# A hybrid mLSTM and retention block on one core: first norm in two parts, scan pieces issued by an account of VectorE and ScalarE

## The chip, the cores and the metric

The kernel runs on one core of one Trainium2 chip. The metric is the device time of one execution in microseconds (us). The median of three runs of the kernel before is 1547.75 us (1546.34 to 1549.2). The engines are named as in the profile: PE is TensorE, DVE is VectorE, ACT is ScalarE, POOL is GpSimd and SP is SyncE, whose queue issues most of the loads and stores.

## What is computed

One layer over a stream of 16 learned meta tokens and 1024 frames of width 1024, in float32. The input is normalised, projected, run through four mLSTM heads (0 to 3) and four retention heads (4 to 7), and projected back; a gated feed-forward part with causal convolutions follows. Cut to what matters:

```python
def token_mixer(u, ...):                       # u: normalised stream
    proj = up @ w_in                           # q, k, v, gate o, input and forget gates
    qk = silu(causal_dwconv(concat(ml_q, ml_k), ml_conv_w))
    h_ml = mlstm_chunkwise(q, k, v, li, lf)    # heads 0-3: decay tables from the gates
    h_ml = sigmoid(ml_o) * head_norm(h_ml)
    h_rt = retention_chunkwise(rotary(rt_q), rotary(rt_k), rt_v, log_gamma)   # heads 4-7
    h_rt = silu(rt_g) * head_norm(h_rt)
    return concat(h_ml, h_rt) @ w_out

h = concat(meta, x)
h = h + token_mixer(rmsnorm(h, norm_mix_g), ...)
u = rmsnorm(h, norm_ffn_g)
h = h + (silu(causal_dwconv(u @ w_up)) * (u @ w_gate)) @ w_down
return rmsnorm(h, norm_final_g)[:, N_META:]
```

## The kernel before

**Dense products.** Each float32 operand of the large products is split into a rounded high part and a low remainder, and a product is three matmuls: high by high (L729), low by high (L730), high by low (L731). `parts` makes the split of a weight: a cast on ACT (L334), a subtraction on DVE (L339). The projections use a seven-product scheme on halves of both operands; the halves of the stream and their sums (S1 to S4, made by `usum` and split by `usplit`, L1551) are its left sides, sums of weight halves its right sides. PSUM banks of a finished product are added into their targets by `evac` (L793): ACT copies or DVE adds (L795, L797, L799). The pairs of letters in the names are the kind of projection: pq for queries and keys, pv for values of a pair of heads, po for the output gate (its target is sig), x and y for the two output halves.

**The stages.** The stream's first norm and head 4's own q, k and v come first (`first_norm`, `v4_group`, `q4_group`), in column ranges of 144, 128, 256, 272 and 256 (r = 0 to 4). Then the order of heads is 4, 0, 1, 2, 3, 5, 6, 7; the dense steps of one head run beside the scan of the head before it. Then follow w_out (about 720 us on), the up and gate products (about 880 on) and the down product.

**The scan.** Each head has nine chunks (16 columns, then eight of 128). `scan_a` makes the scores s of a chunk and from them kw (ACT) and the masked scores pt (DVE); `scan_b` makes the state update u and the output n, and with DVE the next state C. After a third of the chunks, `post_steps` takes the statistics for the head norm (bn, mv, z), scales the values (ACT, into v4lo and v4hi for head 4), and transposes them (tr); DVE multiplies by the gate (mx) and SP stores the result. For heads 0 to 3 the decay tables A1 and A2 are loaded from a scratch array by `tables_load` (L908), and `tables_tasks` (L924) adds the mask on DVE (L931, L932) and takes the exponential on ACT. `qk_tasks` makes convolution, silu or rotary of the next head's q and k.

**What sets the order.** The program deals these pieces out between the dense steps. `watch` keeps an account of each engine's time, `load`, from the sizes of the instructions issued. `slot` issues one dense step of 12 matmuls, first letting the waiting generators (`front`, `pend`) go on by a step, then taking pieces from the list `side`. A piece that uses TensorE has a condition, and is taken when the instructions that it rests on have been issued: their names are in the set `done`. Pieces that are left at the end of a stage are issued by `drain` without dense steps between them. Tile's scheduler makes the final order of each engine from this. Raw weights are loaded on SP's queue by jobs into four slots; `w_unit` (L474) makes sums of two row blocks of w_out and stores them for later.

**The first norm.** `rms` (L665) multiplies the squared stream by a column of ones to get sums per column (pca), takes the root on ACT and the reciprocal on DVE (rcola), and spreads the result over the partitions by a product with the identity (pra). `first_norm` (L692) squares and adds, calls `rms`, scales the stream by it and splits it into u11h, u11l and so on.

## Time and profile before

| | |
|---|---|
| median of three runs | 1547.75 us |
| the profiled execution | 1548.18 us, span 1546.4 us |
| PE busy | 1497.8 us (97%), 9917 matmuls |
| DVE busy | 1080.8 us (70%) |
| ACT busy | 766.1 us (50%) |
| POOL busy | 74.3 us (5%) |
| HBM | 178.05 MB read, 67.15 MB written |

The rows shown further down are of the profiled execution. A row of the view of waits reads: engine, what waited, what it waited for, microseconds in total, times, longest. A row of the timeline has start, duration, engine, line, operation, output and inputs, shape, count, and in brackets the idle time ahead of it with what ended it. Tile numbers are left out of names there: tr, n, u, s, C, A are those of whichever head is at work. Busy time of PE is modelled, since matmuls are pipelined.

### The profile page before, as it was taken

Reading aid. Unit: us, or ns where it says so; the run is one execution under the profiler, and the core shown is the slowest. Engines: PE = TensorE matmul, PEld = TensorE weight load, DVE = VectorE, ACT = ScalarE, POOL = GpSimd, SP = SyncE. Lnnn points to the kernel's source line nnn. Section 1 sums busy time; section 2 is a strip of 40 time slices with the busy share of each in tenths; the row PEclk is TensorE's granted clock in tenths of the full one; section 3 lists DMA queues with packets and bytes.
Section 4 is the critical chain, followed back from the end, with each engine's and each line's share of the span. In section 5 each row is a group of like instructions: output and inputs, shape, how many; then the busy total and the mean of one; then the engine's idle time right before and its main releaser. Section 6 shows DMA issues by size and latency. Waiting matters only on the chain.

```text
span 1546.4 us, 25487 instructions
## 1 busy us (share of the span) xinstructions
PE 1497.8 (97%) x9917; PEld 1353.0 (87%) x9917; DVE 1080.8 (70%) x2112; ACT 766.1 (50%) x1464; POOL 74.3 (5%) x133
## 2 busy tenths in 40 slices
PE   6999799999999999999999999999999999999997
PEld 5999689999889999997888988999999999888887
DVE  7885667667667567755768778666666666778657
ACT  5564565565555446543445455444444444434443
POOL 1000000000000000000000001222220000000000
PEclk9999899999999999999999999999999999999999
DMA  6132146223533354589333228887773223933313
GB/s 243 42 110 71 41 112 216 78 87 116 186 112 101 103 186 166 196 309 337 103 109 132 87 78 241 206 210 199 190 185 89 82 82 128 381 110 112 98 43 110
DMA packets 104585, 223.79 MB, mean 145 GB/s; under 512 B 10520, under 2 KB 33760, under 8 KB 104288
## 3 DMA queue, kind: packets, MB, share of 16 engines
q1 hardware_dynamic: 95872, 199.02, 38.7%
q0 software_dynamic: 8448, 23.07, 7.5%
q8 instruction: 77, 1.26, 0.3%
q14 instruction: 44, 0.36, 0.1%
q10 hardware_dynamic: 144, 0.07, 0.0%
HBM read 178.05 MB, written 67.15 MB: 159 GB/s over the span
## 4 chain that ended last, share of the span: by engine, by line
PE 80%; DVE 4%; DMA 4%; ACT 3%; issue 1%; SPq 0%; DVEq 0%; ACTq 0%
PE pdx L731 3%; PE pdx L730 3%; PE pdx L729 3%; PE pup_x L730 2%; PE pup_x L731 2%; PE pga_x L729 2%; PE pup_x L729 2%; PE pga_x L730 2%; PE pga_x L731 2%; PE pdy L731 2%; PE pdy L730 2%; PE pdy L729 2%; PE pwx L731 2%; PE pwx L729 2%; PE pwx L730 2%; PE n L1366 2%
## 5 line engine op out<-in xcount | busy, mean ns | idle before, releaser
L628 ACT CAST hi_up<-raw_up 128x512 fp32r<-128x512 f32 (+1 forms) x52 | 36.4, 719 | 107.4 <-PE pga_z L730 61.1
L629 DVE TENSOR_TENSOR lo_ga<-fraw_ga,hi_ga 128x512 fp32r<-128x512 f32 (+1 forms) x52 | 41.8, 808 | 38.8 <-ACT hi_ga L628 38.6
L729 PE MATMUL pup_x<-uh_g,hi_up 128*128 128x256 f32 (+1 forms) x240 | 67.2, 283 | 1.2 <-ACT uh_g L1688 1.2
L730 PE MATMUL pup_x<-ul_g,hi_up 128*128 128x256 f32 (+1 forms) x240 | 67.4, 282 | 0.1
L629 DVE TENSOR_TENSOR lo_up<-raw_up,hi_up 128x512 fp32r<-128x512 f32 (+1 forms) x52 | 41.3, 809 | 37.4 <-ACT hi_up L628 36.6
L731 PE MATMUL pup_x<-uh_g,lo_up 128*128 128x256 f32 (+1 forms) x240 | 66.4, 282 | 0.0
L629 DVE TENSOR_TENSOR lo_d<-rd,hi_d 128x1024 fp32r<-128x1024 f32 (+1 forms) x34 | 37.7, 1112 | 32.8 <-ACT hi_d L628 32.7
L628 ACT CAST hi_ga<-fraw_ga 128x512 fp32r<-128x512 f32 (+1 forms) x52 | 36.4, 719 | 46.5 <-PE pup_z L730 22.7
L731 PE MATMUL pdx<-uh_d,lo_d 128*128 128x512 f32 (+1 forms) x156 | 57.9, 375 | 0.0
L730 PE MATMUL pdx<-ul_d,hi_d 128*128 128x512 f32 (+1 forms) x156 | 57.8, 374 | 0.0
L628 ACT CAST hi_d<-rd 128x1024 fp32r<-128x1024 f32 (+1 forms) x34 | 32.3, 959 | 49.3 <-PE pdy L730 32.5
L731 PE MATMUL pdy<-uh_d,lo_d 128*128 128x512 f32 x132 | 51.9, 393 | 0.0
L730 PE MATMUL pdy<-ul_d,hi_d 128*128 128x512 f32 x132 | 51.7, 392 | 0.0
L729 PE MATMUL pdx<-uh_d,hi_d 128*128 128x512 f32 (+1 forms) x156 | 48.5, 372 | 0.0
L729 PE MATMUL pdy<-uh_d,hi_d 128*128 128x512 f32 x132 | 47.9, 389 | 0.0
L729 PE MATMUL pga_x<-uh_g,hi_ga 128*128 128x512 f32 x120 | 47.5, 396 | 0.0
L730 PE MATMUL pga_x<-ul_g,hi_ga 128*128 128x512 f32 x120 | 47.5, 396 | 0.0
L729 PEld LDWEIGHTS pup_x<-uh_g,hi_up 128*128 128x128 f32 x240 | 45.3, 189 | 2.3 <-ACT uh_g L1688 1.4
L731 PE MATMUL pga_x<-uh_g,lo_ga 128*128 128x512 f32 x120 | 47.1, 393 | 0.0
L730 PEld LDWEIGHTS pup_x<-ul_g,hi_up 128*128 128x128 f32 x240 | 45.4, 189 | 1.0 <-DVE ul_g L1689 0.3
L731 PEld LDWEIGHTS pup_x<-uh_g,lo_up 128*128 128x128 f32 x240 | 44.7, 189 | 0.8
L509 POOL DMA_DIRECT2D wsd<-w_down_d x33 | 19.7, 733 | 471.6 <-DVE s2up L1916 471.2
(1688 smaller groups left out, 5779.7 us busy)
## 6 DMA issues: line engine op xcount, KB each, us to landing
raw_up<-w_up_d SPq DMA_DIRECT2D x22, 512.0 KB, 4.3
fraw_ga<-w_gate_d SPq DMA_DIRECT2D x22, 512.0 KB, 4.4
acts<-cv SPq DMA_DIRECT2D x44, 256.0 KB, 4.3
wsd<-w_down_d POOLq DMA_DIRECT2D x44, 256.0 KB, 6.8
rd<-wsd SPq DMA_DIRECT2D x22, 512.0 KB, 3.5
raw_w<-w_out_d SPq DMA_DIRECT2D x20, 512.0 KB, 5.6
wsw<-raw_w SPq DMA_DIRECT2D x32, 256.0 KB, 2.0
raw_m<-w_out_d SPq DMA_DIRECT2D x14, 512.0 KB, 4.5
```

What stands on the lines that cost most here:

```text
L509: dep(G.dma_start(x, y), last["pace"], True)
L628: AC.copy(hi[:, o:o + n], x)
L629: V.tensor_tensor(lo[:, o:o + n], x, hi[:, o:o + n].bitcast(F32), ALU.subtract)
L729: m.append(PE.matmul(pt, ah, xh_, start=first and k == 0, stop=False, skip_group_check=True))
L730: PE.matmul(pt, ah, xl_, start=False, stop=False, skip_group_check=True)
L731: m.append(PE.matmul(pt, al, xh_, start=False, stop=last and k == n - 1, skip_group_check=True))
L1366: PE.matmul(pn[:L, :nv], pt[:L, :L], v, start=True, stop=c == 0)
```

## The change

It has these parts.

1. **The first norm.** `first_norm` is cut in two: `norm_sums` (squares, column sums, root, reciprocal) and `norm_split` (spread, scale, split), and `rms` into `rms_sums` and `rms_rows`. The sums of a range are called one group of products ahead of its scaling. A range with a remainder takes one root and one reciprocal for all its columns instead of two; the second range gives its eight squares to TensorE unsummed.
2. **Head 4's values.** In `v4_group` the high part of the stream goes through both parts of the weights before its low part is used, and the second range's sums can be called between.
3. **Splits.** The subtractions of S3 and S4 in `usplit` run on GpSimd instead of DVE.
4. **The first `w_unit`** moves from ahead of head 4's gate to a place behind it.
5. **The issue rule.** `done` holds, with each name, the time on the account at which DVE and ACT are through with it; a piece is taken when PE's account has reached it. `tr` is such a name for the bank of the transposes. Waiting generators in `pend` pause while DVE or ACT is more than 3 us ahead of PE's account. A change of the activation table is charged 1.3 us to ACT. `tables_tasks` waits until PE's account is 9 us behind `tables_load`.

```diff
+    TABLES = ("Sqrt", "Sigmoid", "Silu", "Exp")
+    table = [None]
     def watch(ins):
...
+        if nm == "Activation":
+            f = ins.func.name if hasattr(ins, "func") else "Copy"
+            if f in TABLES and f != table[0]:
+                table[0] = f
+                load[nm] += 1.3
...
             for g in list(q):
+                if q is pend and not rush[0] and max(load["DVE"], load["Activation"]) - load["PE"] > 3:
+                    break
                 if next(g, pend) is pend:
...
-    done = set()
+    class Ready(dict):
+        def add(self, key):
+            self[key] = max(load["DVE"], load["Activation"]) + 0.3
+        def discard(self, key):
+            self.pop(key, None)
+        def can(self, *keys):
+            return all(k in self and (rush[0] or load["PE"] >= self[k]) for k in keys)
+    done = Ready()
...
+        done["tr"] = load["DVE"] + 0.9
...
-                while "meta" in done:
+                while "meta" in done or dealt[0] and not done.can("tr"):
                     yield
...
-        if k == 0:
-            ask(js)
...
-                if k:
-                    ask(js, True)
+                ask(js, True)
...
-    for f in w_units(1):
-        f()
-    u_fm("o", 4, *v_units(0, 0))
+    u_fm("o", 4, *v_units(0, 0), *w_units(1))
...
+    def norm_sums(r):
...
         if r < 2:
-            V.tensor_tensor(sq[1], xs[1], xs[1], ALU.mult)
+            m = V.tensor_tensor(sq[1], xs[1], xs[1], ALU.mult)
+            if r:
+                after(m, last["scale"])
...
+        if r == 1:
+            ss = [x[:, k] for x in sq for k in range(4)]
+        else:
+            V.tensor_tensor(sq[0], sq[0], sq[1], ALU.add)
+            V.tensor_tensor(sq[0][:, 0:2], sq[0][:, 0:2], sq[0][:, 2:4], ALU.add)
+            ss = [sq[0][:, k] for k in range(2)]
+        norms[r] = xs, rms_sums(ss[0], 0, n, f"a{r}", ..., "tr", ss[1:])
...
-        for i, j in ((0, 0), (1, 0), (0, 1)):
+        for i, j in ((0, 0), (0, 1), (1, 0)):
+            if i and between:
+                between()
...
+        tabs["at"] = load["PE"]
...
         def make():
+            while not rush[0] and load["PE"] < tabs["at"] + 9:
+                yield
...
+        done.add(("pre", h, c))
...
-            return lambda: {("qk", h, int(c > 4))} | ({("tab", h)} if h < H else set()) <= done and not (h == 7 and "meta" in done)
+            return lambda: done.can(("qk", h, int(c > 4)), *([("tab", h)] if h < H else [])) and not (h == 7 and "meta" in done)
...
-            return lambda: (h, c) in pre and (set(turn) <= done if c == 0 else ("n", h, c - 1) in done)
+            return lambda: (h, c) in pre and done.can(("pre", h, c), *(turn if c == 0 else [("n", h, c - 1)]))
...
-    first_norm(0)
+    norm_sums(0)
     v0_split()
+    norm_split(0)
+    v4_group(1, next(ring0), lambda: norm_sums(1))
     need(("q4", 0), 1)
-    v4_group(1, next(ring0))
+    norm_split(1)
     v4_group(0, next(ring0))
-    first_norm(1)
     v4_group(2, next(ring0))
-    first_norm(2)
+    norm_sums(2)
...
-            V.tensor_tensor(l_, part(x, i), h_.bitcast(F32), ALU.subtract)
+            (G if nm in ("S3", "S4") else V).tensor_tensor(l_, part(x, i), h_.bitcast(F32), ALU.subtract)
```

How the instructions move is shown at three places; a row has the line, the operation, output and inputs, shape and count, and lines are numbered by each kernel's own text. First TensorE at the end of head 4's scan, where pv0x1 and pv0y0 are dense products, u4, s4 and n4 the scan's, and tr4_1 the transposes of its second third. Before:

```order
L731 MATMUL pv0x1_1606<-hi_vp0_4_0_1823,uS3l_856 128x256
L1364 MATMUL u4_7_1593<-v4hi_207,kw4_7_1566 128x256
L1317 MATMUL s4_8_1589<-qT4_920,kT4_921 128x128
L1366 MATMUL n4_7_1595<-v4hi_207,pt4_7_1559 128x256
L1368 MATMUL n4_7_1595<-C4_6_1569,qT4_920 128x256
L1366 MATMUL n4_8_1621<-v4hi_207,pt4_8_1591 128x256
L1368 MATMUL n4_8_1621<-C4_7_1600,qT4_920 128x256
L1421 MATMUL tr4_1_0_1704<-cs_73,v4lo_206 128x128
L1421 MATMUL tr4_1_0_1704<-cs_73,v4hi_207 128x128 x2
L1421 MATMUL tr4_1_1_1708<-cs_73,v4lo_206 128x128
L1421 MATMUL tr4_1_1_1708<-cs_73,v4hi_207 128x128 x2
L729 MATMUL pv0y0_1653<-hi_vp0_5_0_1907,uS4h_883 128x256
```

and with the change, where the first rows are those around the first transposes and the dots stand for dense products alone:

```order
L1403 MATMUL n4_7_1556<-v4hi_207,pt4_7_1488 128x256
L1405 MATMUL n4_7_1556<-C4_6_1512,qT4_908 128x256
...
L761 MATMUL pv0x1_1620<-lo_vp0_2_0_1683,uS2h_611 128x256
L1458 MATMUL tr4_1_0_1638<-cs_73,v4lo_206 128x128
L762 MATMUL pv0x1_1620<-hi_vp0_2_0_1682,uS2l_612 128x256
L1458 MATMUL tr4_1_0_1638<-cs_73,v4hi_207 128x128
L760 MATMUL pv0x1_1620<-hi_vp0_2_0_1682,uS2h_611 128x256
...
L1403 MATMUL n4_8_1583<-v4hi_207,pt4_8_1536 128x256
L1405 MATMUL n4_8_1583<-C4_7_1562,qT4_908 128x256
...
L1458 MATMUL tr4_1_1_1667<-cs_73,v4lo_206 128x128
L1458 MATMUL tr4_1_1_1667<-cs_73,v4hi_207 128x128 x2
```

The run of scan products and transposes is broken up by 15 dense products behind n4_7, 16 more ahead of n4_8 and 18 more ahead of tr4_1_1.

Second DVE where head 1 gets its table A1_1, while head 0's gate product (po0, into sig) is emptied out of PSUM. Before:

```order
L931 TENSOR_TENSOR A1_1_2495<-A1_1_2495,mask_118 128x16
L339 TENSOR_TENSOR lo_q1_1_0_2448<-raw_q1a_2292,hi_q1_1_0_2447 128x512 x2
L416 TENSOR_TENSOR raw_q1a_2292<-raw_q1a_2292 128x512
L1383 BN_STATS bn0_7_2411<-v0_01_2138 128x6
L799 TENSOR_TENSOR sig_110<-sig_110,po0x0_2202 128x256
L932 TENSOR_TENSOR A1_1_2495<-A1_1_2495,mask_118 128x1024
L417 TENSOR_TENSOR raw_q1a_2292<-raw_q1a_2292,raw_q1b_2352 128x512
L799 TENSOR_TENSOR sig_110<-sig_110,po0x1_2236 128x256
L1384 BN_AGGR mv0_2_2396<-bn0_7_2411 128x2
L1355 MEMSET mv1_0_2973 128x2
L799 TENSOR_TENSOR sig_110<-sig_110,po0y0_2263 128x258
```

and with the change:

```order
L832 TENSOR_TENSOR sig_110<-sig_110,po0y1_2221 128x256
L1372 TENSOR_TENSOR pt0_8_2487<-s0_8_2485,A1_0_1642 128x128
...
L1437 SCALAR_TENSOR_TENSOR z0_1_2515<-z0_1_2515,mv0_1_2324 128x3
L1414 SCALAR_TENSOR_TENSOR C0_7_2520<-C0_6_2460,dec_115,u0_7_2510 128x257
L967 TENSOR_TENSOR A1_1_2616<-A1_1_2616,mask_118 128x16
L1420 BN_STATS bn0_7_2524<-v0_01_2088 128x6
L507 TENSOR_TENSOR raw_w9_2470<-raw_w9_2470,raw_w1_2468 128x512
L1443 RECIPROCAL z0_1_2515<-z0_1_2515 128x3
L968 TENSOR_TENSOR A1_1_2616<-A1_1_2616,mask_118 128x1024
L1421 BN_AGGR mv0_2_2509<-bn0_7_2524 128x2
L1444 SCALAR_TENSOR_TENSOR mv0_1_2324<-mv0_1_2324,z0_1_2515 128x3
L832 TENSOR_TENSOR rawq_102<-rawq_102,pq1y0_2602 128x264
```

The last evacuation of po0 now stands ahead of the mask's two additions, and the next evacuation behind them is one of pq1.

Third TensorE at the start, where pca is a column sum, pra the spread root, and pv4 head 4's values. Before:

```order
L673 MATMUL pca0_224<-cs_73,sqr0_132 16x1 x2
L673 MATMUL pca0_224<-cs_73,sqr0_132 128x1 x2
L685 MATMUL pra0_233<-cs_73,rcola0_223 128x16
L685 MATMUL pra0_233<-cs_73,rcola0_223 128x128
L767 MATMUL pv4_1_271<-w0hiq_106,u11h_124 128x264 x4
L767 MATMUL pv4_1_271<-w0hik_107,u12h_126 128x264 x4
L755 MATMUL pv4_0_298<-w0raw0_104,ug_117 32x264 x4
L767 MATMUL pv4_1_271<-w0hiq_106,u11l_125 128x264 x4
```

and with the change:

```order
L688 MATMUL pca0_220<-cs_73,sqr0_132 128x1 x4
L700 MATMUL pra0_231<-cs_73,rcola0_219 128x16
L700 MATMUL pra0_231<-cs_73,rcola0_219 128x128
L688 MATMUL pca1_268<-cs_73,sqr0_132 128x1 x4
L800 MATMUL pv4_1_248<-w0hiq_106,u11h_124 128x264 x4
L688 MATMUL pca1_268<-cs_73,sqr1_133 128x1 x4
L800 MATMUL pv4_1_248<-w0hik_107,u12h_126 128x264 x4
L800 MATMUL pv4_1_248<-w0lo0_108,u11h_124 128x264 x4
```

The second range's sums, now eight products instead of two, stand around the first group of values instead of behind it.

66 lines of the change are left out of this document (37 added, 29 removed).

## The prediction

> **What bounds the kernel now.** I read the head of the page first, then TensorE's busy time in stretches of the span, then what it waited for, then the clock in the stretches behind a wait. The profiled execution took 1548.18 us, 0.43 above the median of the three runs; its span is
>
> ```profile
> span 1546.4 us, 25487 instructions
> ```
>
> so 1.8 us lie outside it. By stretches (length, then busy time and instructions of PE, its weight loads, DVE, ACT, POOL; then PE's granted clock, DMA share and GB/s):
>
> ```profile
> core 0: us, PE busy (x) PEld busy (x) DVE busy (x) ACT busy (x) POOL busy (x), PEclk, DMA share, GB/s
> 0.00:20.00 20.00, 9.34 (x53) 6.91 (x54) 12.30 (x32) 11.70 (x19) 5.64 (x8) 1.00 0.96 326
> 20.00:40.00 20.00, 17.45 (x131) 16.80 (x131) 19.43 (x46) 9.85 (x18) 0.00 (x0) 0.91 0.40 152
> 40.00:80.00 40.00, 40.00 (x342) 39.09 (x341) 34.48 (x53) 22.05 (x36) 3.36 (x2) 1.00 0.13 37
> ...
> 150.00:180.00 30.00, 21.58 (x129) 18.62 (x127) 21.27 (x49) 19.22 (x36) 0.11 (x1) 0.83 0.14 45
> ...
> 222.00:235.00 13.00, 8.72 (x60) 7.93 (x59) 8.11 (x22) 10.68 (x22) 0.18 (x1) 0.93 0.44 161
> ...
> 300.00:320.00 20.00, 18.08 (x127) 17.22 (x126) 14.05 (x38) 15.22 (x30) 0.74 (x2) 0.91 0.18 54
> ...
> 395.00:410.00 15.00, 11.92 (x83) 11.35 (x82) 9.45 (x21) 11.20 (x21) 0.00 (x0) 0.89 0.53 166
> ...
> 720.00:740.00 20.00, 16.45 (x68) 12.51 (x67) 13.67 (x24) 4.81 (x7) 0.00 (x0) 0.91 0.64 219
> ...
> 960.00:1500.00 540.00, 540.00 (x3066) 473.07 (x3065) 365.71 (x552) 233.72 (x397) 50.81 (x72) 1.00 0.54 154
> ...
> sum 1546.40, PE 1497.84 PEld 1352.98 DVE 1080.78 ACT 766.11 POOL 74.33; mean PE 74.89 PEld 67.65 DVE 54.04 ACT 38.31 POOL 3.72
> ```
>
> TensorE sets the time: 1497.84 of 1546.4 us busy, and not idle at all from 960 to 1500. A change that leaves its products alone can win only the 48.6 us of idle and what is run at a low clock behind it. The change reorders two places: the first norm (10.66 + 2.55 us idle up to 40 us) and the scan of the heads, where 8.42, 4.28, 1.92 and 3.08 us are idle in four short stretches, 17.7 us together. The 3.55 at 720 to 740 stand in a part whose order on TensorE stays as it was. In those four stretches it waited for:
>
> ```profile
> PE tr L1421 <- ACT v4lo L1412: 3.8, 1, 3.8
> PE tr L1421 <- DVE mx L1429: 2.6, 1, 2.6
> PE n L1366 <- ACT v4hi L1379: 1.4, 1, 1.4
> ...
> PE pq1y L729 <- ACT sig L795: 2.0, 1, 2.0
> PE po0x L729 <- DVE sig L799: 1.6, 1, 1.6
> ...
> PE pq2x L729 <- DVE rawk L799: 1.9, 1, 1.9
> ...
> PE pq3y L729 <- ACT sig L795: 1.8, 1, 1.8
> PE pq3x L729 <- DVE sig L799: 1.3, 1, 1.3
> ```
>
> The first three are the end of head 4's scan: the last scan products and the transposes (tr) of its output follow one another with nothing dense between, so each waits out the chain of the other engines. The other five are dense products that wait for a PSUM bank which DVE or ACT has not emptied. What DVE did instead, at the second stretch, by its timeline and, for the other two, by its waits:
>
> ```profile
> 218.66 0.17 DVE L931 TENSOR_TENSOR A<-A,mask 128x16 f32<-128x16 f32 x1 [3.94 <-DMA A<-scr]
> ...
> 222.97 1.23 DVE L932 TENSOR_TENSOR A<-A,mask 128x1024 f32<-128x1024 f32 x1 [1.65 <-DMA A<-scr]
> ...
> 225.15 0.42 DVE L799 TENSOR_TENSOR sig<-sig,po0y 128x258 f32<-128x258 f32 x1
> ```
> ```profile
> DVE A L931 <- DMA A<-scr: 2.9, 1, 2.9
> ...
> DVE A L931 <- DMA A<-scr: 2.7, 1, 2.7
> ```
>
> DVE stood still for the decay table of the next head, with the evacuations of L799 queued behind it. And after each gap TensorE's clock was about half for a while:
>
> ```profile
> 174.35:178.57 4.22, 4.21 (x20) 4.22 (x21) 2.60 (x7) 3.87 (x6) 0.00 (x0) 0.51 0.13 47
> ...
> 233.16:236.40 3.24, 3.24 (x14) 3.24 (x15) 1.12 (x2) 2.86 (x6) 0.00 (x0) 0.50 0.76 229
> ...
> 315.26:318.80 3.54, 3.54 (x19) 3.28 (x19) 2.36 (x7) 3.54 (x12) 0.18 (x1) 0.55 0.00 0
> ...
> 403.90:406.50 2.60, 2.60 (x13) 2.60 (x13) 1.63 (x3) 1.27 (x3) 0.00 (x0) 0.50 0.56 180
> ```
>
> Length times (1 − clock) gives 2.07 + 1.62 + 1.59 + 1.30 = 6.6 us, which the busy share hides. The four places cost 17.7 + 6.6 = 24.3 us.
>
> **The scan's new issue rule.** A piece of the scan is now put out only when the account of DVE and ACT says that its inputs are done, and not by the fact that their instructions were issued. At the end of head 4 the new order has 15 dense products between its seventh n and the first transpose, 16 more before the last n and 18 more before the last transposes, where before there were none; one dense product takes about 0.11 us (4.22 us hold 20 at 0.51 of the clock), so each of these runs is 1.7 to 2 us. The waits were 3.8, 1.4 and 2.6 us, 7.8 together, for chains that began one after the other; 49 products are 5.3 us, and the chains now also overlap. I put the whole first stretch down as removed: −8.42 − 2.07 = −10.5.
>
> **The tables.** The mask additions are held back by 9 us of TensorE's account behind the issue of their load. The waits of 3.94 + 1.65, 2.9 and 2.7 us on that load are all below 9. In the new order of DVE all four evacuations of head 0's gate (po0) stand ahead of the mask, and the next one behind it is of pq1. For heads 1 and 3 this takes away what the waits rest on; for head 2 the last evacuation of pq2 still stands behind the mask, with products between that ask for it later. Removed: (4.28 + 1.62) + (1.92 + 1.59) + (3.08 + 1.30) = −13.8. If the table is late even so, DVE's next state update (C) and the evacuation behind it are late, and one such place costs its old price, 3.5 to 5.9 us.
>
> [...]
>
> **New waits.** Each change of the activation table is now charged to ACT, which only delays pieces; the new order has one more reload near the end of head 4. The raw weights of head 0's gate (raw_o0b) are now loaded behind a store of head 4's output on SP's queue, and the first w_out pair (two loads, four additions on DVE, four stores) is moved out of the prologue into that stage; on DVE the addition that needs raw_o0b stands in front of the state C and the masked scores pt that head 4's last chunk needs. Bounds: nothing (the load has landed), or 3.9 us of DVE, the longest such wait above, with the 31 dense products ahead of that chunk's n (3.3 us) as cover. I leave one of the four places in at about the middle of its price, +4.5; none is the lower bound, two the upper (+9).
>
> **The first norm.** Rows of the timeline, of TensorE, of DVE, of ACT and of POOL:
>
> ```profile
> 7.07 1.21 PE L673 MATMUL pca<-cs,sqr 128*16 128x1 f32 x8 [7.07 <-DVE sqr L703]
> ...
> 18.43 0.61 PE L673 MATMUL pca<-cs,sqr 128*128 128x1 f32 x4
> ...
> 23.73 0.75 PE L767 MATMUL pv<-w0hiq,u11h 128*128 128x264 f32 x4 [1.80 <-ACT u11h L709]
> ```
> ```profile
> 4.90 0.76 DVE L699 TENSOR_TENSOR sqr<-x 128x576 f32<-128x576 f32 x1 [3.84 <-DMA x<-h_in_d]
> ...
> 10.17 1.17 DVE L699 TENSOR_TENSOR sqr<-x 128x512 f32<-128x512 f32 x1 [1.26 <-DMA x<-h_in_d]
> ```
> ```profile
> 23.59 1.06 ACT L701 ACTIVATE sqr<-x 128x1024 f32<-128x1024 f32 x1
> ```
> ```profile
> 8.37 2.42 POOL L737 TENSOR_TENSOR w0lo<-w0raw,w0hiq 128x1056 fp32r<-128x1056 f32 x1 [7.44 <-ACT w0hiq L736]
> 10.76 2.86 POOL L737 TENSOR_TENSOR w0lo<-w0raw,w0hik 128x1056 fp32r<-128x1056 f32 x1
> ```
>
> The first chain loses a square root, a reciprocal and, by moving the second group's square (1.17) behind the scaling, up to 1.1 us on DVE; against that both casts of w0 (1.05 more of ACT) now stand ahead of the root. Hence −0.7 to 0 for the first dense product. The second group's column sums are 8 products instead of 2, in the trace 4 records of 0.61 us; 12 records more are at 0.13 to 0.15 each 1.6 to 1.8 us of TensorE, part of it inside the 1.80 us wait before u11h. That wait itself moves later: on DVE the sum of the fourth group's squares now stands ahead of the second group's scaling, and on ACT the square at 23.59 (1.06 us) ahead of the cast to u11h. As that chain starts 0.3 to 0.5 us earlier, I put 0.5 to 0.8 us down for it. Bounds of the whole part: −0.7 (gain kept, the sums hidden) and +2.6 (all sums and the delay on the path). The four additions taken off DVE, in a stretch where it is 19.43 of 20 us busy, speak for the low half; I take +0.6.
>
> **The splits on GpSimd.** Four subtractions of 128x1056 leave DVE (two of S3 stand here) for POOL:
>
> ```profile
> 75.11 2.41 DVE L1556 TENSOR_TENSOR uS3l<-x,uS3h 128x1056 fp32r<-128x1056 f32 x2
> ```
>
> That is 4.9 us less on DVE and, by the two rows of POOL, 4 × 2.4 to 2.9 = 10 to 11 us there. From 40 to 80 TensorE never waited, with DVE 34.48 of 40 us busy, so DVE's gain is worth nothing by itself. POOL's load is not free for DVE: the square beside it took 1.17 us for 512 columns, the one alone 0.76 for 576. So 0.4 us for each DVE instruction that overlaps, at most the 10 to 11 us less the 4.9 saved: 0 to +6 us of DVE, covered as long as the weights of the gate product lie ahead. I take 0. [...]
>
> **The sum.** 1548.2 − 10.5 − 13.8 + 4.5 + 0.6 = 1529.0 us. With no place left in and the prologue's lower bound it is 1523, with two left in and the upper bound 1535.5: that is this case's own range.
>
> **Rivals.**
> *Half is given back* (chance 0.22). The account only knows nominal durations; where DVE really is behind, the dense products between the pieces wait for PSUM banks in place of the transposes. For it: in the first stretch DVE is 21.27 of 30 us busy, and head 0's twelve convolution steps still stand between the transposes' users. Against it: the evacuations lie ahead of the table now. [...]
> *It does not do what it says* (0.08). The pieces move, but what is late is the table's DMA and DVE's own backlog, and the stalls only move along: 1546 to 1549. For it: all three later stretches have the same DMA behind them. Against it: DVE was idle there and no longer has to stand still.
> *The held-back pieces pile up* (0.13): slower. Accounts that are too pessimistic hold every head's scan back; what is left over when the dense steps of a stage are dealt out is issued in one go, without dense products between. The first stretch shows the price: two chunks and two pairs of transposes cost 8.42 + 2.07 = 10.5 us, so about 5.2 for one chunk with its transposes. If one chunk more is left at each of seven heads this is 7 × 5.2 = 36.7 us: 1548.2 − 24.3 + 36.7 + 0.6 = 1561. It decides from five heads on (26 us). For it: the new order has twelve or more dense products between the pieces of head 0's chunks, so that its scan takes more of the stage than before. Against it: in the new order every head's last n products still have dense products between them, and from the sixth head on the order is almost the old one.
>
> **How the numbers follow.** The forecast has 0.57, the rivals 0.22, 0.08 and 0.13. A measurement of this kernel can tell about 0.2%, 3.1 us, from no change. The third case splits into half no change, a quarter faster, a quarter slower; with some of the pile-up near zero: faster 0.57 + 0.22 + 0.01 = 0.80, same 0.06, slower 0.14. The range runs from 1522, just under the best case of the forecast, through the second case to 1545; above it lie the pile-up and most of the third case, below it little, 2 in 10 together.
>
> **What would show it.** Right: at head 4's end no wait of a tr product above 0.5 us; at the places where head 1, 2 and 3 get their tables no wait of a dense product for sig or rawk; PEclk 1.00 through the scan; TensorE's idle down from 48.6 to about 28. In the prologue the first pv at 12.5 to 13.2 and the second u11h wait ending near 24.5. Wrong: waits of po, pq or pv products for L799's successors in head 4's stage, DVE waiting for raw_o0b or A, or scan products in unbroken rows at a stage's end. From the table of w_out on, at 720 us, each wait should be found again as it was; if the difference arises there, the reasoning above is beside the point.

## The result and the profile after

The change takes 1551.62 us (median of 20 runs, 1548.01 to 1556.14) against 1548.83 us (20 runs, 1546.34 to 1554.4) for the kernel before on the same chip: ratio 1.0013, 95% interval 1.0001 to 1.0024. That is about 2 us slower, and less than the 0.2% that the prediction took as the least difference that can be told; 1529.0 was forecast.

The profiled execution took 1552.23 us, 4.05 more than that of before.

The stretches of the changed kernel, with the columns of the prediction's table of stretches (PE, its weight loads, DVE, ACT, POOL, PE's granted clock, DMA share, GB/s):

```profile
core 0: us, PE busy (x) PEld busy (x) DVE busy (x) ACT busy (x) POOL busy (x), PEclk, DMA share, GB/s
0.00:40.00 40.00, 29.19 (x153) 26.91 (x154) 28.47 (x68) 20.35 (x32) 5.18 (x8) 0.87 0.63 221
80.00:125.00 45.00, 35.14 (x253) 32.75 (x251) 35.70 (x72) 25.45 (x45) 11.74 (x6) 0.89 0.28 89
150.00:185.00 35.00, 35.00 (x274) 33.92 (x273) 26.47 (x60) 25.98 (x48) 0.11 (x1) 1.00 0.27 84
222.00:240.00 18.00, 18.00 (x138) 16.41 (x133) 9.53 (x28) 12.77 (x20) 0.37 (x2) 1.00 0.60 185
240.00:262.00 22.00, 18.18 (x142) 17.10 (x141) 15.23 (x36) 14.37 (x31) 0.51 (x2) 1.00 0.66 212
300.00:320.00 20.00, 19.31 (x139) 18.13 (x138) 13.26 (x33) 10.26 (x21) 0.57 (x3) 1.00 0.33 104
395.00:430.00 35.00, 32.33 (x242) 30.99 (x241) 23.79 (x61) 27.31 (x50) 0.40 (x2) 0.95 0.64 203
720.00:740.00 20.00, 16.33 (x67) 12.58 (x66) 13.81 (x27) 6.29 (x11) 0.00 (x0) 0.83 0.76 263
```

The stretch from 80 to 125, of which nothing was predicted, read thus in the kernel before:

```profile
80.00:125.00 45.00, 44.33 (x362) 43.17 (x361) 35.38 (x82) 25.11 (x48) 0.21 (x2) 1.00 0.32 109
```

Two things stand out. The 8.42 us of idle at the end of head 4's scan (150 to 185) are gone, as forecast. And a stretch in which TensorE had waited 0.67 us now has 9.86 us of idle and a clock of 0.89: 253 products where there were 362. TensorE's idle time in all is 46.5 us (1550.4 less 1503.9 busy), where the prediction had 48.6 fall to about 28. In the view of TensorE's waits of the changed kernel (what waited, for what, us in total, times, longest) the new entries are these:

```profile
PE pq0x L760 <- ACT rawq L828: 3.4, 1, 3.4
PE pe L1079 <- DVE gsm L1075: 3.0, 1, 3.0
PE po4x L760 <- ACT sig L828: 2.5, 1, 2.5
...
PE pq1x L760 <- ACT rawq L828: 2.2, 1, 2.2
PE pq3x L760 <- ACT rawq L828: 2.2, 1, 2.2
...
PE pq1x L760 <- DVE rawk L832: 1.1, 1, 1.1
```

The first three lie between 80 and 125. The last three are the heads' table places once more, with other tiles: pq1 and pq3 wait where po0, pq1 and pq3 did.

What a place costs is taken here as its idle time plus its busy time times one minus the granted clock, an estimate from the columns of the stretches. Summed that way over slices of 1 us (so the clock is taken where it was low; rows of whole stretches give a little less), in us, one profile each, less than 0.4 shown as 0:

| stretch | before | after | rule alone | both splits alone | S3's split alone | splits + norm | rule + S3's split |
|---|---|---|---|---|---|---|---|
| first po4x product starts at | 73.5 | 78.2 | 74.7 | 72.7 | 74.6 | 75.7 | 74.9 |
| lost 80–125 | 0.7 | 14.6 | 0.8 | 10.5 | 8.1 | 14.5 | 11.5 |
| lost 125–150 | 0.5 | 1.0 | 0 | 0.5 | 0 | 4.0 | 0 |
| lost 150–185 (head 4's end) | 11.6 | 0 | 11.8 | 0 | 0 | 0 | 0 |
| lost 222–262 (table of head 1) | 5.9 | 3.8 | 4.8 | 2.3 | 2.4 | 3.7 | 8.0 |
| lost 300–430 (heads 2, 3) | 8.4 | 5.0 | 4.8 | 3.4 | 4.3 | 8.1 | 6.1 |
| lost 600–740 | 5.3 | 6.3 | 5.4 | 5.2 | 6.4 | 6.0 | 5.4 |
| span | 1546.4 | 1550.4 | 1543.8 | 1536.7 | 1536.8 | 1551.8 | 1547.4 |

For the change: +4.7 in the prologue (the first po4x product comes that much later), +13.9 at 80 to 125, +0.5, −11.6 at head 4's end, −2.1 and −3.4 at the tables, +1.1 at 720, +1.0 of small waits between 430 and 580: +4.1, the difference of the two profiled executions. The other columns are the experiments.

How far one profile can be trusted is shown by two of the experiments below that turned out to be the same program as another one, instruction for instruction (the rule with and without its hold; S3's split with and without the hold). Between the two profiles of one program the start of po4x differs by 1.2 and 2.0 us, and an entry of the table by up to 2.0 us (4.3 and 6.3 at 300 to 430); their ratios differ by 0.0007 and 0.0005. So the entries at 80 to 125 and at head 4's end stand far above the scatter; the prologue's +4.7 and the single places behind 125 do not. Two columns are also not typical of their kernel: the profiled execution of both splits alone was the fastest of its six, 4.8 us below their median, and that of rule + S3's split the slowest of its eleven, 4.1 above.

### The profile page after: what moved, and what is told of

It reads as the page before. It is cut to its first block, busy times and chain, and to the rows that moved or that the text cites. A ratio compares the mean times of both kernels' runs of the same rounds, so it can differ in the third digit from the quotient of the medians.

```text
span 1550.4 us, 25495 instructions
## 1 busy us (share of the span) xinstructions
PE 1503.9 (97%) x9929; PEld 1361.5 (88%) x9929; DVE 1080.2 (70%) x2103; ACT 772.2 (50%) x1467; POOL 83.8 (5%) x137
## 4 chain that ended last, share of the span: by engine, by line
PE 85%; DMA 7%; DVE 4%; ACT 3%; issue 1%; SPq 0%; DVEq 0%; ACTq 0%
PE pdx L762 3%; PE pdx L761 3%; PE pdx L760 3%; PE pup_x L761 2%; PE pup_x L762 2%; PE pup_x L760 2%; PE pga_x L760 2%; PE pga_x L761 2%; PE pga_x L762 2%; PE pdy L762 2%; PE pdy L761 2%; PE pdy L760 2%; PE pv L800 2%; PE pwx L762 2%; PE pwx L760 2%; PE pwx L761 2%
```

## The experiments

Each ratio is against the kernel before on the same chip in the same session, with its 95% interval; 0.1% is 1.55 us. They came in four groups.

### Which part moved head 4's end

Only the rule, with the old norm and the subtractions back on DVE (the moved pair of w_out stays):

```diff
-    norm_sums(0)
+    first_norm(0)
...
-            (G if nm in ("S3", "S4") else V).tensor_tensor(l_, part(x, i), h_.bitcast(F32), ALU.subtract)
+            V.tensor_tensor(l_, part(x, i), h_.bitcast(F32), ALU.subtract)
```

> Both undone: only the issue rule, the table account, the 9 us hold and the moved first pair of w_out rows are left. If the two costs add up: 1535 to 1541 us, 8 to 14 below the kernel before. Rival (the new waits between 80 and 125 and at head 1's queries belong to the rule): 1546 or more.

Measured: 1548.38 us, 0.998 (0.9968 to 0.9993). A stretch and two waits of this kernel:

```profile
150.00:185.00 35.00, 26.39 (x161) 22.46 (x159) 25.52 (x60) 20.55 (x39) 0.21 (x2) 0.85 0.31 102
```
```profile
PE tr L1441 <- ACT v4lo L1432: 4.0, 1, 4.0
PE tr L1441 <- DVE mx L1449: 2.9, 2, 2.6
```

In time the rival is right, but not in its reason: it gave the new waits between 80 and 125 to the rule, and by the table the rule alone loses 0.8 us there. What is left at head 4's end is 35 − 26.39 = 8.61 us of idle at 0.85, the old stall with its old waits (3.8 and 2.6 before). The rule does not touch it.

Only the splits: in the kernel before, the subtractions of S3 and S4 on GpSimd and nothing else.

```diff
-            V.tensor_tensor(l_, part(x, i), h_.bitcast(F32), ALU.subtract)
+            (G if nm in ("S3", "S4") else V).tensor_tensor(l_, part(x, i), h_.bitcast(F32), ALU.subtract)
```

> The kernel before with only the subtractions of S3 and S4 moved to GpSimd. Theory: DVE loses 8 to 11 us between 75 and 100 us, TensorE waits for lo_o and for PSUM, and the time rises by 6 to 12 us, to 1555 to 1561. Rival (DVE has room there, as the prediction took it): within 1.5 us of 1548.8.

Measured: 1543.52 us, 0.9945 (0.9928 to 0.9961): faster, where the theory had slower by several us; the theory fell. Its stretches:

```profile
80.00:125.00 45.00, 37.65 (x278) 35.99 (x277) 34.40 (x78) 24.76 (x48) 5.20 (x4) 0.92 0.40 119
150.00:185.00 35.00, 35.00 (x270) 33.14 (x269) 28.54 (x67) 22.52 (x42) 0.39 (x3) 1.00 0.24 77
```

Both marks of the changed kernel are here without the rule and without the norm: no idle at head 4's end, 7.35 us at 80 to 125. The whole change with the subtractions back on DVE is the counter-test:

```diff
-            (G if nm in ("S3", "S4") else V).tensor_tensor(l_, part(x, i), h_.bitcast(F32), ALU.subtract)
+            V.tensor_tensor(l_, part(x, i), h_.bitcast(F32), ALU.subtract)
```

> The changed kernel with the subtractions of S3 and S4 back on DVE. Theory (GpSimd's subtractions hold DVE back): lo_o beside uS3l and the gate steps beside uS4l return from 2.5-2.7 us each to 0.3-1.3, the loads of raw_q0a go out some 8 us earlier, and most of the 9.9 us of idle and 4.8 us of low clock between 80 and 125 us go: 1540 to 1545 us, against 1551.6. Rival (head 4's scan and its gate chain are dealt out too early by the issue rule): the idle time between 80 and 125 stays within 2 us of 9.9, and the time within 2 us of 1551.6.

Measured: 1552.11 us, 1.0001 (0.9992 to 1.0011).

```profile
80.00:125.00 45.00, 43.35 (x359) 41.60 (x360) 37.03 (x88) 26.41 (x49) 0.10 (x1) 1.00 0.32 101
150.00:185.00 35.00, 26.17 (x162) 23.12 (x161) 25.45 (x62) 21.90 (x40) 0.10 (x1) 0.80 0.29 98
```

The stall at 80 to 125 goes, as the theory had it, and the stall at head 4's end comes back (8.83 us at 0.80), which it had not. What the splits do can be counted in TensorE's order, from the last n of chunk 7 of head 4 to the last transpose of its second third, and how many products of any kind stand ahead of the first gate product pe of head 0:

```
                              dense products between   ahead of pe
before                                  0                  667
rule alone                              0                  660
norm alone                              0                  673
change, splits on DVE                   0                  666
both splits alone                      51                  534
S3's split alone                       50                  534
rule + both splits, old norm           65                  535
the change                             49                  541
```

With a subtraction on GpSimd about 130 dense products move from ahead of head 0's gates to behind them, and some 50 of them come to lie in head 4's last products. Neither the rule nor the norm did that, and not the kernel's own account, from which the subtractions vanish when DVE no longer makes them: built with GpSimd's subtractions charged to DVE the order keeps its 51 and 50 dense products, built with DVE's left uncharged it keeps its 0. What is left is Tile's scheduler, which makes the final order. The numbers that instructions get as the program issues them say the same: by these numbers the 9456 products of the kernel before and of both splits alone come in one and the same order, with 484 ahead of pe, and only the final orders differ. So the 11.6 us gained at 150 to 185 come from dense products that the scheduler moved, and so does a part of the loss at 80 to 125: cover taken from the gates of head 0 and given to the end of head 4. How large that part is stays open (see "What stays open" below).

The change with the old norm and the old order of head 4's values:

```diff
-    norm_sums(0)
+    first_norm(0)
...
-        for i, j in ((0, 0), (0, 1), (1, 0)):
+        for i, j in ((0, 0), (1, 0), (0, 1)):
```

> The changed kernel with the first norm, the order of head 4's values and the calls at the start as before. Theory (the split norm costs time: extra column sums and 10 us at half clock from 26 to 36.5 us): the first gate product starts near 73.5 us again instead of 78.2, and the time falls by about 4 to 5 us, to 1547. Rival (what the start loses is taken up by slack later): within 1.5 us of 1551.6.

Measured: 1543.17 us, 0.9948 (0.9934 to 0.9963), against 1.0013 for the whole change: the new norm costs 10 us there, more than the theory said. At 80 to 125 it is 6.64 us idle instead of 9.86:

```profile
80.00:125.00 45.00, 38.36 (x290) 36.62 (x288) 33.98 (x75) 23.44 (x44) 6.68 (x5) 0.92 0.41 117
```

The time equals that of the splits alone (0.9945): beside both splits the rule gains nothing.

### What the rule does

The rule alone, without the account's times (a piece is taken when its inputs have been issued, as before; the hold on the mask, the pause of `pend` and the charge for tables stay):

```diff
-            return all(k in self and (rush[0] or load["PE"] >= self[k]) for k in keys)
+            return all(k in self for k in keys)
...
-                while "meta" in done or dealt[0] and not done.can("tr"):
+                while "meta" in done:
```

> The issue rule without its times: old norm, splits on DVE, names counted as done when issued; the table account, the pause, the 9 us hold and the moved w_out pair are kept. Theory (the times slow the scan down, so that the last use of a head's table, and with it the next table's load, come some 15 us later, and the waits of 2.2 us for rawq follow from that): the table of head 1 is loaded near 215 us, not 230, the wait for rawq goes, and the time is 2 to 5 us below the rule alone. Rival (the times are what removes the stalls of the heads): 2 us or more above it.

The rule alone, without the hold of 9 us:

```diff
-            while not rush[0] and load["PE"] < tabs["at"] + 9:
-                yield
```

> The issue rule with its times but without the 9 us hold of the table's mask. Theory of the prediction (the hold takes the evacuations out from behind the mask): the stalls of 2 to 4 us for sig at heads 1 and 3 return, 3 to 6 us above the rule alone. Rival (the scan's slower pace has already moved the mask behind the evacuations): within 1.5 us of it.

Measured: 1547.59 us, 0.9981 (0.9968 to 0.9994), and 1549.3 us, 0.9987 (0.9972 to 1.0002). All three forms of the rule lie together, so neither theory of the first run holds in time (2 to 5 us below the rule alone, or 2 above). The waits without the times differ, though:

```profile
PE pq3x L745 <- DVE sig L815: 2.5, 2, 1.6
PE pq1x L745 <- DVE sig L815: 2.4, 2, 1.3
```

Without the hold:

```profile
PE pq1x L745 <- ACT rawq L811: 2.7, 1, 2.7
PE pq3x L745 <- ACT rawq L811: 2.2, 1, 2.2
```

Without the times the old kind of wait, for DVE's sig, is back, and the load of head 1's table goes out near its old time, on SP's queue of this kernel:

```profile
216.76 0.33 SPq L938 DMA_DIRECT2D A<-scr  x1
```

Without the hold everything is as with it, and it has to be: built, the rule with the hold and the rule without it have the same instructions in the same order on every engine. What moves the mask are the times: in the order of DVE all six evacuations of po0 stand ahead of head 1's mask in every kernel that has the times, and two to four of them in those that have not. So the times do what was meant to be the hold's work, by another way. Rows of the changed kernel's DVE, of SP's queue, of ACT and of TensorE (start, duration, then as in the timelines above):

```profile
229.22 0.28 DVE L1372 TENSOR_TENSOR pt<-s,A 128x128 f32<-128x128 f32 x1
...
236.83 1.23 DVE L968 TENSOR_TENSOR A<-A,mask 128x1024 f32<-128x1024 f32 x1 [2.18 <-DMA A<-scr]
```
```profile
229.53 0.32 SPq L955 DMA_DIRECT2D A<-scr  x1
```
```profile
237.94 1.28 ACT L974 ACT_TABLE_LOAD   x1
...
241.60 1.56 ACT L974 ACTIVATE A<-A,cols 128x128 f32<-128x128 f32 x5
...
244.35 0.37 ACT L828 COPY rawq<-pq1x 128x264 f32<-128x264 f32 x1
```
```profile
244.78 0.39 PE L760 MATMUL pq1x<-uS2h,hi_q 128*128 128x264 f32 x1 [2.23 <-ACT rawq L828]
```

and the same two steps in the kernel before, on DVE and on SP's queue:

```profile
214.44 0.28 DVE L1336 TENSOR_TENSOR pt<-s,A 128x128 f32<-128x128 f32 x1
```
```profile
214.75 0.33 SPq L921 DMA_DIRECT2D A<-scr  x1
```

The scan of head 0 is held to a slower pace, so its last pt, which is the last reader of the old table, comes at 229.22 instead of 214.44, and the load of the next one 0.3 us behind it. By 236 the evacuations of po0 are over, and DVE's wait for the mask costs nothing. What is late next is ACT: the exponentials of the table and the load of ACT's function table for them make 3.8 of the 6.4 us from 237.94 to the copy of pq1x at 244.35 (scaled values and two casts of weights make most of the rest), and TensorE waits 2.23 us for the bank.

Both splits, old norm, without the times:

```diff
-            return all(k in self and (rush[0] or load["PE"] >= self[k]) for k in keys)
+            return all(k in self for k in keys)
...
-    norm_sums(0)
+    first_norm(0)
```

> As e6, with the subtractions of S3 and S4 on GpSimd. If the two gains add (head 4's scan end covered by dense products that the splits hold back; tables loaded early and their mask held): 1536 to 1541 us, below the splits alone. Rival (both act on the same stalls): 1542 to 1546, like the splits alone.

Measured: 1542.02 us, 0.9953 (0.9938 to 0.9968), the same as with the times (0.9948) and as the splits alone (0.9945); nothing is lost at head 4's end. That settles it from the other side: the stall goes without the account's times.

### What the norm does

The new norm and values order alone, in the kernel before:

```diff
-    first_norm(0)
+    norm_sums(0)
     v0_split()
+    norm_split(0)
+    v4_group(1, next(ring0), lambda: norm_sums(1))
```

> The kernel before with the new first norm alone (and the new product order of head 4's values). Theory (the norm's new order costs time by narrow products and longer stretches at half clock): the first gate product starts 2 to 5 us later, and the time is 3 to 5 us above the kernel before. Rival (the norm costs only together with the splits on GpSimd): within 1.5 us of it.

Measured: 1551.51 us, 1.0008 (0.9996 to 1.002): by itself about +1.2 us, not to be told from no change. The same norm edit with both splits in the kernel before, without the rule:

```diff
-    first_norm(0)
+    norm_sums(0)
...
-            V.tensor_tensor(l_, part(x, i), h_.bitcast(F32), ALU.subtract)
+            (G if nm in ("S3", "S4") else V).tensor_tensor(l_, part(x, i), h_.bitcast(F32), ALU.subtract)
```

> The kernel before with the splits on GpSimd and the new first norm, without any of the issue rule. Theory (the norm eats the splits' gain, whatever the rule): 1549 to 1553 us. Rival (the norm is only costly together with the rule, whose held-back pieces it delays): 1543 to 1546, like the splits alone plus 1 or 2.

Measured: 1552.78 us, 1.0023 (1.0013 to 1.0033): 12 us above the splits alone, and level with the whole change. So the norm and both splits spoil each other, with or without the rule, and by the table above over many places: 3.0 us in the prologue, 4.0 at 80 to 125, 3.5 at 125 to 150, 1.4 and 4.7 at the tables. (The two profiles lie 15 us apart and not 12, since that of the splits was their fastest execution.)

Two parts of the norm were undone in the whole change. The second range's squares added on DVE, two column sums instead of eight:

```diff
-        if r == 1:
+        if False:
             ss = [x[:, k] for x in sq for k in range(4)]
```

> The whole change, but the second range's eight squares are added on DVE and summed by two products, like the other ranges. Theory (the narrow products cost their own 1.6 us and keep the clock low): the stretch at half clock behind 26 us shortens by some 4 to 6 us, and the time falls by 3 to 5 us below the whole change. Rival (the low clock comes from the wait at 25 us alone): within 1.5 us of the whole change less 1.6.

and head 4's values in the old order of products:

```diff
-        for i, j in ((0, 0), (0, 1), (1, 0)):
-            if i and between:
-                between()
+        for i, j in ((0, 0), (1, 0), (0, 1)):
...
-    v4_group(1, next(ring0), lambda: norm_sums(1))
+    norm_sums(1)
+    v4_group(1, next(ring0))
```

> The whole change, but head 4's values take their products in the order of before (high by high, low by high, high by low). Theory (this order is not what costs): within 1.5 us of the whole change. Rival (the new order runs more of the wide products at half clock, since they come before the clock has risen): 3 us or more below it.

Measured: 1547.01 us, 0.9981 (0.9973 to 0.999), so 5 us of the change were in the eight sums; and 1551.08 us, 1.0009 (0.9999 to 1.002), so the order of the values is not it. But the 5 us did not come back in the prologue, as the theory had it: in that profile po4x starts at 77.2, 1.0 earlier than in the change, and the loss at 80 to 125 is 12.0 instead of 14.6. Both differences are of the size of the scatter between profiles of one program. What does differ is the order: with two sums 63 dense products lie in head 4's last products, with eight 49. A few narrow products at the start again move the order that follows; where the 5 us come from is not shown.

For the prologue alone, the start of the first po4x product is the measure. In the ten kernels with the old norm it is 72.7 to 76.6, mean 74.2; in the five with the whole new norm 75.3 to 78.3, mean 76.9. The norm costs about 2.7 us there, one profile each.

### Less of the splits

The kernel before with S3's subtraction alone on GpSimd:

```diff
-            V.tensor_tensor(l_, part(x, i), h_.bitcast(F32), ALU.subtract)
+            (G if nm == "S3" else V).tensor_tensor(l_, part(x, i), h_.bitcast(F32), ALU.subtract)
```

> The kernel before with only the subtraction of S3 on GpSimd, that of S4 on DVE. The order of TensorE at head 4's end is then that of both splits on GpSimd; the time that DVE is held is halved. Theory (the gain comes from the order, the loss from the held DVE): the stall at head 4's end is gone, idle time between 80 and 125 us is 2 to 5 us less than with both, and the time is 1538 to 1543, at or below both. Rival (the gain comes from DVE's load): half the gain of both, 1545 to 1548.

Measured: 1537.73 us (6 runs, 1536.48 to 1542.01), 0.9925 (0.9913 to 0.9938). It beats both kernels and every other program here. Its stretch from 80 to 125:

```profile
80.00:125.00 45.00, 40.20 (x299) 37.92 (x291) 35.05 (x81) 25.43 (x53) 1.75 (x3) 0.92 0.40 119
```

One pair of subtractions is enough for the new order: 50 dense products at head 4's end, and no loss there by the table; and without the second pair 2.6 us less are idle at 80 to 125. The two gate steps of DVE that both pairs stretch (see below) take 0.28 and 0.41 us here, and pe no longer waits for gsm; but the next product of that chain, pf, now waits 2.2 us for it.

The whole change with S4's subtraction back on DVE, that is S3's alone on GpSimd:

```diff
-            (G if nm in ("S3", "S4") else V).tensor_tensor(l_, part(x, i), h_.bitcast(F32), ALU.subtract)
+            (G if nm == "S3" else V).tensor_tensor(l_, part(x, i), h_.bitcast(F32), ALU.subtract)
```

> The whole change with only the subtraction of S3 on GpSimd, that of S4 on DVE. Theory (the norm costs more beside the splits because S4's subtraction then holds DVE just when the gate chain and the queries' weights are due): the 9.9 us of idle between 80 and 125 fall below 6, and the time is 1540 to 1546. Rival (the norm's cost lies in its own order and in the waits for rawq at pq0, whatever DVE does): 1547 to 1552.

and the same with the old norm, so the rule and S3's split:

```diff
-    norm_sums(0)
+    first_norm(0)
```

> S3's subtraction on GpSimd with the issue rule and the old norm. Theory (the rule adds nothing once the splits have moved the order): within 2 us of S3 alone, 1536 to 1541. Rival (the rule's gain of some 3 us adds): 1533 to 1536.

Measured: 1545.91 us, 0.9974 (0.9962 to 0.9986), and 1545.08 us, 0.9968 (0.9957 to 0.9979). The first came out in time as expected, but with 7.8 us still idle at 80 to 125. Both theories missed the second: beside S3's split the rule costs (0.9968 − 0.9925) × 1550 = 6.7 us, or 5.9 against the 0.993 of the next run, the same program measured in the same session. A stretch of it, and the same stretch with S3's split alone:

```profile
222.00:262.00 40.00, 35.38 (x253) 34.06 (x252) 27.25 (x65) 27.84 (x52) 1.21 (x3) 0.91 0.56 172
```
```profile
222.00:262.00 40.00, 37.64 (x304) 35.05 (x302) 31.09 (x59) 22.94 (x45) 0.21 (x2) 1.00 0.61 199
```

With the rule the place where head 1 gets its table has 4.6 us of idle and a clock of 0.91, without it 2.4 and 1.00. The first of these two stretches is from the slowest of that kernel's executions, so the 8.0 us of the table may be more than it mostly loses there. In sum the rule gains 3 us in the old order, nothing beside both splits and costs 6 to 7 us beside S3's split alone; why it costs there is not shown beyond this stretch.

The last: S3's split with the hold of 9 us on the mask and nothing else of the rule.

```diff
+        tabs["at"] = load["PE"]
...
+            while not rush[0] and load["PE"] < tabs["at"] + 9:
+                yield
```

> The kernel before with S3's subtraction on GpSimd and the 9 us hold of the table's mask, nothing else. Prediction's step (the hold takes the mask out from ahead of the evacuations): the waits for sig at heads 1 and 3 (1.3 to 1.8 us each) go, 3 to 5 us below S3 alone. Rival (9 us of account do not move the mask past the evacuations, since the account is behind by then): the waits stay, within 1.5 us of S3 alone.

Measured: 1539.17 us, 0.993 (0.9916 to 0.9944): as without the hold. Its waits are the old ones:

```profile
PE pq3y L729 <- ACT sig L795: 1.8, 1, 1.8
PE pq1y L729 <- ACT sig L795: 1.7, 1, 1.7
...
PE pq3x L729 <- DVE sig L799: 1.3, 1, 1.3
```

The hold is inert, with the rule and without it: this kernel, too, has instruction for instruction the order that it has without the hold. The same came out where the hold was put into the kernel before, and where it was taken out of the rule without its times, both built and not run.

## Why the prediction was wrong

**The scan's new issue rule, −10.5: the effect was right, its cause was not.** Head 4's end lost its stall, 11.6 us by the slices, and the counts of 15, 16 and 18 dense products were those that ran. But they came from the splits: the rule alone leaves 0 there, the splits alone put 51. The prediction read the whole change's order and gave its most useful move to the part that seemed made for it; that the forecast for this place came true was luck.

**The tables, −13.8: measured −5.5, by another way.** The reason given was that the hold lets the evacuations pass ahead of the mask. The hold changes no instruction. The slower scan makes the load itself late, the mask with it, and then the exponentials stand ahead of ACT's copies: pq1x and pq3x wait 2.2 us each for rawq, pq1x 1.1 more for rawk. The prediction named the state update C as what would be late next; it was ACT. The mark given for a right step, no wait for sig or rawk at these places, was met for sig alone, and a wait for rawq was not on the list.

**New waits, +4.5: 0.** DVE did stand still for raw_o0b, 1.8 us, within its bounds of 0 to 3.9; TensorE had no idle from 150 to 185, so the dense products covered it.

**The first norm, +0.6: about +2.7 in the prologue,** its upper bound of +2.6. The first dense product came at 13.56, against 13.20 before and a forecast of 12.5 to 13.2, and the second wait for u11h ended at 26.49, against 23.73 before and a forecast near 24.5. Beside both splits the norm costs 10 to 12 us, and no bound held that. Why is open.

**The splits on GpSimd, 0 (bounds 0 to +6): the step that decides the sign.** Their price was looked for in DVE's busy time, and set to nothing since the products ahead of the gate product would cover it; the same subtractions made the scheduler move some 130 of these away. By themselves they were worth −8.5 us; in this change, with the new norm ahead of them, they brought a loss of 14.6 us at 80 to 125 (1.7 with the subtractions back on DVE) for the 11.6 at head 4's end. GpSimd's rows in the changed kernel:

```profile
80.38 5.77 POOL L1598 TENSOR_TENSOR uS3l<-x,uS3h 128x1056 fp32r<-128x1056 f32 x2
...
95.28 5.48 POOL L1598 TENSOR_TENSOR uS4l<-s,uS4h 128x1056 fp32r<-128x1056 f32 x2 [9.13 <-ACT uS4h L1597]
```

and DVE beside them:

```profile
81.23 5.47 DVE L358 TENSOR_TENSOR lo_o<-raw_o4b,hi_o 128x512 fp32r<-128x512 f32 x2 [0.27 <-ACT hi_o L353]
...
95.39 2.50 DVE L1072 TENSOR_TENSOR gates<-gates 36x128 f32<-36x128 f32 x1
...
98.42 2.62 DVE L1073 TENSOR_TENSOR_SCAN gates<-gates 36x128 f32<-36x128 f32 x1
```

The same instructions in the kernel before:

```profile
77.45 1.28 DVE L339 TENSOR_TENSOR lo_o<-raw_o4b,hi_o 128x512 fp32r<-128x512 f32 x2
...
102.35 0.28 DVE L1036 TENSOR_TENSOR gates<-gates 36x128 f32<-36x128 f32 x1
102.89 0.41 DVE L1037 TENSOR_TENSOR_SCAN gates<-gates 36x128 f32<-36x128 f32 x1
```

Four DVE instructions grow by 4.19 + 2.22 + 2.21 = 8.6 us, for 4.9 us that DVE saved: 3.7 us net, inside the bounds of 0 to +6, though the 0.4 us that the prediction counted for each instruction is far below the 2.1 to 2.2 measured. The two of the gates stand in the chain to gsm, for which the product pe waits 3.0 us. Each of the four took about as long (2.50 to 2.74 us) as the subtraction beside it on GpSimd (2.74 to 2.89 us). So the prediction looked for the price in the right place, and set it to nothing for cover that it had not checked in the new order.

**The rivals.** The stalls did move along, and at 1551.62 the time is nearest to the case "it does not do what it says" (1546 to 1549), but hardly by its mechanism: DVE waited for the table of head 1 (2.18 us) while no evacuation stood behind it. The pile-up did not come. The sign of the first rival, dense products that wait for PSUM banks, did come (pq0x 3.4, po4x 2.5, pq1x and pq3x 2.2 us each), but its reason, an account that takes DVE to be further than it is, holds at the most for the tables: without the rule, both splits alone wait 2.4 us for po4x and 1.6 for pq0x, and with the new norm 2.3 and 3.4. That an edit of one part sets the scheduler's order of another, which decided, was no rival at all. By themselves the splits make −8.5 us, the rule −3.1 and the norm +1.2, together −10.4, and the three in one kernel +2.0: 12 us are in what they do to each other.

**What stays open.** Why the new norm costs so much with both subtractions on GpSimd (10 us with the rule, 12 without) and hardly with S3's alone (0.9974 against 0.9968 with the rule, 0.9 us) is not settled; with both subtractions on GpSimd and no rule, the counts of the table of orders are nearly the same with the new norm (49 and 541) as without it (51 and 534). Nor is it settled how the loss at 80 to 125 divides between the four stretched DVE instructions (8.6 us) and the cover that moved away, since no kernel had the one without the other. S3's split alone still loses 8.1 us there (7.1 in the other profile of that program), with the gates' instructions at their old length. That speaks for the moved cover, but lo_o is stretched in it as well (5.40 us for the two), so it is argued and not shown.

## What to carry to other kernels

Where a scheduler makes the final order, compare the order with each part of a change applied alone before a moved instruction is credited to a part: the counts of 0 and 51 dense products need no run, nor does the finding that the hold changes nothing. A small operation put on a slower engine (here a subtraction of 2.74 to 2.89 us on GpSimd that took 1.18 to 1.24 on DVE) can be worth more by the order that it brings about than by its own time, and the smallest such edit can be the best (one pair of subtractions, 0.9925); parts that gain alone may lose together, so measure them together and apart. The subtractions on GpSimd had a price here on four DVE instructions beside them, 2.1 to 2.2 us each; look for such a price above all where one of these stands in a chain that TensorE waits for, as those of the gates do here (3.0 us of pe for gsm).

## What the runs showed of the hardware

The low clock did not follow the length of the wait. The cleanest pair is one program profiled twice, S3's split alone and the same with the inert hold. In both, the same product ends nearly the same wait; then the 3.6 us behind it:

```profile
87.18 0.58 PE L729 MATMUL po4x<-uS2h,hi_o 128*128 128x256 f32 x1 [2.41 <-ACT sig L795]
```
```profile
87.20:90.80 3.60, 3.60 (x18) 3.60 (x19) 2.55 (x10) 2.79 (x5) 0.00 (x0) 0.54 0.62 225
```
```profile
89.19 0.39 PE L729 MATMUL po4x<-uS2h,hi_o 128*128 128x256 f32 x1 [2.40 <-ACT sig L795]
```
```profile
89.20:92.80 3.60, 3.60 (x30) 3.59 (x30) 2.56 (x10) 2.70 (x5) 0.00 (x0) 1.00 0.64 217
```

Behind 2.41 us of idle the first has a clock of 0.54 and gets through 18 products, behind 2.40 us the second has 1.00 and gets through 30. In the changed kernel, the stretch behind a wait of 1.83 us, with the product that ended it:

```profile
26.00:36.50 10.50, 10.01 (x47) 10.02 (x48) 10.37 (x24) 3.77 (x8) 0.00 (x0) 0.52 0.02 7
```
```profile
26.49 1.25 PE L800 MATMUL pv<-w0hiq,u11h 128*128 128x264 f32 x4 [1.83 <-ACT u11h L740]
...
27.98 2.55 PE L688 MATMUL pca<-cs,sqr 128*128 128x1 f32 x12
```

There the clock was about half (0.52) for 10.5 us, against 2.6 to 4.2 in the prediction's rows of the kernel before, with twelve products of one column between; whether these prolonged it is not shown. Behind the 2.23 us at 244.78, in a stretch with 3.8 us of idle, it stayed at 1.00. So it was low behind 2.41 and 1.83 us and full behind 2.40 and 2.23; what decides it is not shown. The 1.3 to 2.1 us that the prediction counted for each gap are no fixed price.
